# Two 256-column products against one 512-column product in the MLPs of a two-layer hybrid transformer

## The chip, the cores and the metric

The kernel runs on one NeuronCore of a Trainium2 chip. The metric is the device time of one execution in microseconds, the median over runs. A profile is one execution taken by the hardware profiler; its span runs from the first to the last instruction.

## The reference

256 tokens of width 2048 pass two layers. Layer 0 is a stick-breaking attention and an MLP, layer 1 a sparse attention (compressed, selected and windowed keys with gates) and an MLP. Each sublayer adds to the residual. The change concerns the MLPs alone:

```python
def sqrelu_mlp(h, w1, w2):
    return jnp.square(jax.nn.relu(h @ w1)) @ w2

h = h + sqrelu_mlp(rms_norm(h, mlp_norm_g[layer]), mlp_w1[layer], mlp_w2[layer])
```

w1 is 2048 x 8192 and w2 8192 x 2048, all in float32.

## The kernel before

Every large product keeps float32's accuracy by splitting both operands into a high and a low part in fp32r: (hi + lo)(hi + lo) without lo times lo, so three products per tile. Weights come in chunks of two contraction tiles (KC = 2, 256 rows) by 512 columns (NB). `load` (line 130) issues one DMA of 512 KB on SP's queue into one of five raw buffers; `split` has ScalarE copy the chunk to hi (line 123) and VectorE subtract to lo (line 125), four buffers each. TensorE then works on the chunk.

There are two forms. `chunk_N` (line 145) has the activations as the stationary side, 128 x 128, and 512 columns of the weights moving past: 4 tiles per chunk, 12 products of 512 columns. `chunk_T` (line 162) has the weights as the stationary side and the 256 tokens moving past: 8 tiles per chunk (2 contraction tiles by 4 blocks m of 128 columns), first hi against xhi and hi against xlo for each tile, then lo against xhi for each: 24 products of 256 columns. Its four blocks m share two PSUM banks. Every product loads its stationary side anew.

`mlp` (line 290) runs, for each of four quarters fg of the hidden width, four blocks fb of 512 hidden columns through `proj_T` (eight chunks of `chunk_T`) and evacuates each block: ReLU on ScalarE (line 303), square on VectorE (305), the high part yhi on ScalarE (308), the low part ylo on VectorE (309). Then four blocks nb of 512 output columns go through `chunk_N` with w2 (eight chunks each), and `add_h` (line 259) adds them to the residual h. The norm's factor goes in there, squared; its gain went into x.

PSUM has two pools of four banks: acc for these products, att for attention and for the transposes of `make_x` (line 201), which makes xhi (line 206) and xlo (208) from the residual. `out_proj` (line 272) stands ahead of each MLP, leaves its last blocks in acc banks, adds them with `add_h` (line 257), and spawns `next_x`, which makes the MLP's x; its last parts are made between the MLP's first chunks.

The order of instructions on each engine is fixed at compile time by a planner that takes them by the program's order as their inputs and buffers come free in its own reckoning; only the first products of layer 0 are ordered by hand. On the chip each engine takes its instructions in that order. `pump` lets pieces of spawned work in between the halves of a chunk.

Of the kernel before, what the change touches and what calls it, by code (L numbers as in the profile page):

```python
# [15 lines left out]
P = 128  # L16
T = 256
# [22 lines left out]
def hybrid_kernel(  # L40
# [15 lines left out]
    # The residual stream, and the contraction operands in two exact parts each.  # L56
    h = cpool.tile([P, NT, D], F32, name="h")
    xhi = cpool.tile([P, KD, T], F32R, name="xhi")
    xlo = cpool.tile([P, KD, T], F32R, name="xlo")
# [3 lines left out]
    # Gains on the partitions: rows of the norms' gains, then of the head norms.  # L63
# [5 lines left out]
    # x in parts, each loaded behind the weights' chunk before it  # L69
# [68 lines left out]
    def bank(pool, tag):  # L138
        return pool.tile([P, NB], F32, tag=tag, name=tag)

    def chunk_N(ps, src, k0, n0, first, last, ahi, alo, koff=0, by_token=False):
        """ps[t][tok, 512] += a[k, tok]^T w[k, 512] for KC contraction tiles."""
        hi, lo = src if isinstance(src, tuple) else load_split(src, k0, KC, n0, NB)
        tiles = [(kk, k0 - koff + kk, t) for kk in range(KC) for t in range(NT)]
        mm = lambda a, b, k, t, s, e: nc.tensor.matmul(ps[t], a[:, k, t * P:(t + 1) * P], b, start=s, stop=e)  # L145
        for part in [[x for x in tiles if x[2] == t] for t in range(NT)] if by_token else [tiles]:
            for kk, k, t in part:
                mm(ahi, hi[:, kk, :], k, t, first and kk == 0, False)
                mm(alo, hi[:, kk, :], k, t, False, False)
            pump()  # L150
            for kk, k, t in part:
                mm(ahi, lo[:, kk, :], k, t, False, last and kk == KC - 1)
            pump()

    def chunk_T(ps, src, k0, n0, first, last):
        """ps[m // 2][n, (m % 2, tok)] += w[k, n]^T x[k, tok] for four blocks m of 128 columns."""
        hi, lo = src if isinstance(src, tuple) else load_split(src, k0, KC, n0, NB)
        tiles = [(kk, m) for kk in range(KC) for m in range(NB // P)]

        def mm(w, x, kk, m, s, e):  # L160
            o = ps[m // 2][:, (m % 2) * T:(m % 2 + 1) * T]
            nc.tensor.matmul(o, w[:, kk, m * P:(m + 1) * P], x[:, k0 + kk, :], start=s, stop=e, skip_group_check=True)  # L162

        for kk, m in tiles:
            mm(hi, xhi, kk, m, first and kk == 0 and m % 2 == 0, False)
            mm(hi, xlo, kk, m, False, False)
        pump()
        for kk, m in tiles:
            mm(lo, xhi, kk, m, False, last and kk == KC - 1)
        pump()  # L170

    def proj_N(src, n0):
        ps = [bank(acc, "acc") for _ in range(NT)]
        for k0 in range(0, KD, KC):
            chunk_N(ps, src, k0, n0, k0 == 0, k0 + KC == KD, xhi, xlo)
        return ps
# [7 lines left out]
    def split_evac(hi, lo, src, scale=None):  # L184
        """hi + lo = src (times a per-partition factor), src in PSUM."""
        if scale is None:
            nc.scalar.activation(hi, src, AF.Copy)  # L187
            nc.vector.tensor_tensor(lo, src, hi.bitcast(F32), op=OP.subtract)  # L188
        else:
            nc.scalar.activation(hi, src, AF.Copy, scale=scale)  # L190
            nc.vector.scalar_tensor_tensor(
                lo, src, scale, hi.bitcast(F32), op0=OP.mult, op1=OP.subtract
            )

# [1 line left out]
    def make_x(kp, g0):  # L196
        """x of the contraction tiles kp, kp + 1."""
        ps = bank(att, "att")
        for j in range(2):
            for t in range(NT):  # L200
                nc.tensor.transpose(  # L201
                    ps[:, j * T + t * P:j * T + (t + 1) * P], h[:, t, (kp + j) * P:(kp + j + 1) * P], ident
                )
        gain = lambda j: gT[:, g0 + kp + j:g0 + kp + j + 1]
        for j in range(2):
            nc.scalar.activation(xhi[:, kp + j, :], ps[:, j * T:(j + 1) * T], AF.Copy, scale=gain(j))
        for j in range(2):
            nc.vector.scalar_tensor_tensor(
                xlo[:, kp + j, :], ps[:, j * T:(j + 1) * T], gain(j), xhi[:, kp + j, :].bitcast(F32),
                op0=OP.mult, op1=OP.subtract,  # L210
            )
# [3 lines left out]
    def ssq(layer, i, n):  # L215
        """The squares of part i of n of the residual's columns."""
# [9 lines left out]
    def next_x(layer, nb, g0):  # L226
        """Behind the residual's block nb: the next layer's x and sum of squares."""
        ssq(layer, nb, D // NB)
        for kp in range(nb * (NB // P), (nb + 1) * (NB // P), 2):
            yield  # L230
            make_x(kp, g0)
# [14 lines left out]
    def bcast_rows(rstd):  # L246
        """[tok] on the partitions -> the same row [tok] on every partition, in PSUM."""
# [13 lines left out]
    def add_out(nb, ps, scale, ov):  # L261
        """The last block goes out in parts, the tokens that are done first before the others."""
# [9 lines left out]
    def out_proj(src, layer, g0):  # L272
        """h += y w: the last heads' part of the first two blocks comes behind the others'."""
# [16 lines left out]
    def mlp(l, layer, junk, done, last=None):  # L290
        w1, w2 = mlp_w1[l], mlp_w2[l]
        r2 = None
        for fg in range(DFF // D):
            for fb in range(D // NB):
                ps = proj_T(w1, fg * D + fb * NB)
# [4 lines left out]
                for b in range(2):  # L300
                    k = fb * (NB // P) + 2 * b
                    r = junk.tile([P, NB], F32, tag="relu", name="relu")
                    nc.scalar.activation(r, ps[b], AF.Relu)
                    s = junk.tile([P, NB], F32, tag="sq", name="sq")
                    nc.vector.tensor_tensor(s, r, r, op=OP.mult)
                    hi = yhi[:, k:k + 2, :].rearrange("p k t -> p (k t)")
                    lo = ylo[:, k:k + 2, :].rearrange("p k t -> p (k t)")
                    nc.scalar.activation(hi, s, AF.Copy)
                    nc.vector.tensor_tensor(lo, s, hi.bitcast(F32), op=OP.subtract)  # L309
            for nb in range(D // NB):  # L310
                end = last is not None and fg == DFF // D - 1 and nb == D // NB - 1
                ps = [bank(acc, "acc") for _ in range(NT)]
# [10 lines left out]
    # ================= layer 0: stick-breaking attention =================  # L323
    with tc.tile_pool(name="sbp", bufs=2) as sp:
# [11 lines left out]
        # The first products, with x made beside them: every engine in the order given here.  # L336
# [27 lines left out]
        def evac(dst, ps, i):  # L364
            """dst[d, head, tok] = ps times the factors of q (i = 0) or k (i = 1)."""
# [14 lines left out]
        def causal(ap, n):  # L380
            """Keep where key (partition) < query, else 0; ap is [P, n, P]."""
# [5 lines left out]
        def attention(hg, qT, kT, v):  # L387
            for hp in range(0, HG, 2):
                # Keys on the partitions; z0 of keys 0-127 for all queries, z1 of keys 128-255 for
                # queries 128-255; two heads beside each other.  # L390
# [17 lines left out]
                for i in range(2):  # L408
                    # softplus(z) = max(z, 0) + ln(1 + exp(-|z|)); log_sigmoid(z) = min(z, 0) - ln(...)
# [72 lines left out]
    # ================= layer 1: native sparse attention =================  # L482
    # Four selected blocks of 64 are the whole sequence and the window is wider than it, so both
    # branches see every key up to the query. Keys of a group: two parts of 128 selected, 128 window
    # and 8 compressed keys; queries 0-127 see the first part alone.
    with tc.tile_pool(name="nsa", bufs=2) as ap, ExitStack() as last:
# [13 lines left out]
        # Minus the distances of queries (partitions) and keys, NEG where a key is not seen.  # L500
# [10 lines left out]
        for t in range(NT):  # L511
            for a in range(t + 1):
                # CS n + CL - 1 - query, for the compressed keys n from a CH
# [7 lines left out]
        # The last of the 2 CH columns is no key.  # L521
        nc.gpsimd.memset(dist[1][:, 1, 2 * P + NCMP - CH:], NEG)

        def compress(i, cT):
# [24 lines left out]
            # gelu(a) = a / (1 + exp(-2 sqrt(2/pi) (a + 0.044715 a^3)))  # L549
# [39 lines left out]
        def heads(pv, t, n):  # L589
            """The n heads [tok, n, d] of rstd * pv, normed."""  # L590
# [11 lines left out]
        def heads_T(hn, n):  # L602
            """Transposed: [d, n, tok], in PSUM."""
# [18 lines left out]
        def scores(g, j, t, q, khi, klo, sums):  # L622
            """exp of head j's biased scores less their maxima, and the sums, of the three branches."""
# [22 lines left out]
        def scale(g, t, pr, sums):  # L646
            """Each branch's gate over its sum, into its probabilities."""
# [12 lines left out]
        def values(g, t, pr, v):  # L660
            """The sum over the branches of p v, keys on the partitions."""
# [73 lines left out]
        # gates: the last 128 columns, of which the last 48 are the gates  # L735
# [24 lines left out]
        # Queries before the end of the first compressed block see none of them.  # L760
# [5 lines left out]
        # the columns of one group: its selected keys and values, its window keys and values  # L766
# [66 lines left out]
```

## Time and profile before

| what | value |
|---|---|
| median of 3 runs | 2268.32 us (2268.23 to 2268.54) |
| span of the profiled execution | 2265.5 us, 34377 instructions |
| TensorE products busy | 2254.0 us, 99%, 13972 products |
| weight loads busy (overlap the products) | 2014.3 us, 89% |
| VectorE busy | 1245.8 us, 55% |
| ScalarE busy | 1071.5 us, 47% |
| HBM traffic | 178 GB/s over the span |

Busy time of TensorE is modelled at the products' ends, so products overlap in the records; what tells their pace is the length of a run of products over their number. A releaser in square brackets in the timeline names what ended the idle time ahead of an instruction. The profiled execution's own time is not given apart from its span; the median of the runs stands 2.8 us above the span.

### The profile page before, as it was taken

What the parts mean: (1) busy time and instruction counts of PE and PEld (TensorE: products, weight loads), DVE (VectorE), ACT (ScalarE), POOL (GpSimd) and SP (SyncE); (2) the same over time, 40 slices, a digit from 0 to 9 for tenths busy, and PEclk for the clock granted to TensorE, in tenths of its full rate; (3) what the DMA queues carried; (4) which work ended last, traced back from release to release, by engine and by line L of the source; (5) the groups of instructions that cost most, each with busy time, mean ns of one, the idle gap of its engine ahead of it and who ended that gap; (6) DMA issues with size and microseconds to landing.
All of it is one profiled execution on the core that took longest, in us unless ns stands there. A gap on an engine that the chain in (4) does not pass through costs nothing.

```text
span 2265.5 us, 34377 instructions
## 1 busy us (share of the span) xinstructions
PE 2254.0 (99%) x13972; PEld 2014.3 (89%) x13972; DVE 1245.8 (55%) x1515; ACT 1071.5 (47%) x1467; POOL 43.1 (2%) x75
## 2 busy tenths in 40 slices
PE   8999999999999999999999999999999999999999
PEld 8999988998998898898898888889989988988987
DVE  5555555555555455555555777755554555554554
ACT  6555565443444344344433666654434443443442
POOL 0000000000000000000000011000000000000000
PEclk9999999999999999999999999999999999999999
DMA  7555545655655665665566544445556656656654
GB/s 244 179 164 169 167 167 180 178 186 191 184 183 189 185 184 187 188 185 187 184 188 199 148 144 135 137 161 184 186 186 188 185 187 186 186 186 187 186 197 137
DMA packets 244375, 406.17 MB, mean 179 GB/s; under 512 B 13172, under 2 KB 59128, under 8 KB 244216
## 3 DMA queue, kind: packets, MB, share of 16 engines
q1 hardware_dynamic: 243432, 403.53, 57.0%
q8 instruction: 109, 1.79, 0.3%
q10 hardware_dynamic: 784, 0.45, 0.1%
q14 instruction: 50, 0.41, 0.0%
HBM read 401.83 MB, written 2.10 MB: 178 GB/s over the span
## 4 chain that ended last, share of the span: by engine, by line
PE 99%; DMA 0%; DVE 0%; SPq 0%; issue 0%; DVEq 0%
PE acc L145 51%; PE acc L162 43%; PE att L682 1%; PE att L201 1%; PE att L543 1%; PE att L674 0%; PE att L675 0%; PE att L676 0%; PE att L442 0%; PE att L394 0%; PE att L628 0%; PE att L630 0%; PE att L629 0%; DMA h<-in_x_dram 0%; PE att L606 0%; PE att L395 0%
## 5 line engine op out<-in xcount | busy, mean ns | idle before, releaser
L125 DVE TENSOR_TENSOR lo<-raw,hi 128x1024 fp32r<-128x1024 f32 x754 | 922.0, 1224 | 853.2 <-ACT hi L123 840.5
L123 ACT ACTIVATE hi<-raw 128x1024 fp32r<-128x1024 f32 x754 | 799.1, 1060 | 1116.1 <-PE acc L145 572.3
L162 PE MATMUL acc<-xhi,hi 128*128 128x256 f32 x2688 | 659.0, 283 | 0.0
L162 PE MATMUL acc<-xlo,hi 128*128 128x256 f32 x2688 | 656.8, 282 | 0.0
L162 PEld LDWEIGHTS acc<-xlo,hi 128*128 128x128 f32 x2688 | 508.1, 189 | 0.5
L162 PEld LDWEIGHTS acc<-xhi,hi 128*128 128x128 f32 x2688 | 507.9, 189 | 0.6
L145 PE MATMUL acc<-hi,yhi 128*128 128x512 f32 x1280 | 507.9, 397 | 0.0
L145 PE MATMUL acc<-hi,ylo 128*128 128x512 f32 x1280 | 503.9, 394 | 0.0
L162 PE MATMUL acc<-xhi,lo 128*128 128x256 f32 x2688 | 375.7, 282 | 0.0
L145 PE MATMUL acc<-lo,yhi 128*128 128x512 f32 x1280 | 350.9, 395 | 0.0
L162 PEld LDWEIGHTS acc<-xhi,lo 128*128 128x128 f32 x2688 | 343.7, 189 | 0.0
L145 PEld LDWEIGHTS acc<-hi,yhi 128*128 128x128 f32 x1280 | 241.0, 188 | 56.5 <-ACT yhi L187 0.2
L145 PEld LDWEIGHTS acc<-lo,yhi 128*128 128x128 f32 x1280 | 240.3, 188 | 56.3 <-issue 0.4
L145 PEld LDWEIGHTS acc<-hi,ylo 128*128 128x128 f32 x1280 | 241.0, 188 | 54.3 <-DVE ylo L188 0.2
L145 PE MATMUL acc<-hi,xhi 128*128 128x512 f32 x384 | 153.1, 399 | 0.0
L145 PE MATMUL acc<-hi,xlo 128*128 128x512 f32 x384 | 151.5, 395 | 0.0
L145 PE MATMUL acc<-lo,xhi 128*128 128x512 f32 x384 | 106.8, 400 | 0.0
L145 PEld LDWEIGHTS acc<-hi,xhi 128*128 128x128 f32 x384 | 72.4, 188 | 15.8 <-ACT hsq L592 0.2
L145 PEld LDWEIGHTS acc<-hi,xlo 128*128 128x128 f32 x384 | 72.4, 188 | 15.3
L145 PEld LDWEIGHTS acc<-lo,xhi 128*128 128x128 f32 x384 | 70.0, 189 | 15.1 <-issue 1.1
L259 DVE SCALAR_TENSOR_TENSOR h<-acc,r,h 128x512 f32<-128x512 f32 x62 | 43.7, 746 | 36.4 <-PE acc L145 36.4
L309 DVE TENSOR_TENSOR ylo<-sq,yhi 128x512 fp32r<-128x512 f32 x64 | 41.2, 685 | 0.0
(182 smaller groups left out, 985.1 us busy)
## 6 DMA issues: line engine op xcount, KB each, us to landing
raw<-in_mlp_w_dram SPq DMA_DIRECT2D x512, 512.0 KB, 3.7
raw<-in_sb_w_qkv_dram SPq DMA_DIRECT2D x96, 512.0 KB, 3.7
raw<-in_nsa_w_in_dram SPq DMA_DIRECT2D x50, 512.0 KB, 3.5
raw<-in_sb_w_out_dram SPq DMA_DIRECT2D x32, 512.0 KB, 3.7
raw<-in_nsa_w_in_dram SPq DMA_DIRECT2D x64, 256.0 KB, 3.2
raw<-in_nsa_w_out_dram SPq DMA_DIRECT2D x32, 512.0 KB, 3.5
w1t<-in_nsa_cmp_w_dram SPq DMA_DIRECT2D x8, 512.0 KB, 4.1
h<-in_x_dram SPq DMA_DIRECT2D x8, 256.0 KB, 7.8
```

Of the source, the lines that this page charges most:

```text
L123: nc.scalar.activation(hi, raw, AF.Copy)
L125: nc.vector.tensor_tensor(lo, raw, hi.bitcast(F32), op=OP.subtract)
L145: mm = lambda a, b, k, t, s, e: nc.tensor.matmul(ps[t], a[:, k, t * P:(t + 1) * P], b, start=s, stop=e)
L162: nc.tensor.matmul(o, w[:, kk, m * P:(m + 1) * P], x[:, k0 + kk, :], start=s, stop=e, skip_group_check=True)
L201: nc.tensor.transpose(ps[:, j * T + t * P:j * T + (t + 1) * P], h[:, t, (kp + j) * P:(kp + j + 1) * P], ident)
L259: nc.vector.scalar_tensor_tensor(hb, ps[t], scale[:, t:t + 1], hb, op0=OP.mult, op1=OP.add)
L309: nc.vector.tensor_tensor(lo, s, hi.bitcast(F32), op=OP.subtract)
L543: nc.tensor.matmul(ph[:, :GC], w1t[:, l - l0, :], blk[:, l, :, :].rearrange("p g n -> p (g n)"), start=l == 0, stop=l == CL - 1,)
L682: nc.tensor.transpose(ptp[:w, j * P:(j + 1) * P], src(j), ident)
```

## The change

xhi and xlo become the halves of one tile xs, `[P, KD, 2, T]`, so that for each contraction tile the 256 tokens of the high part and the 256 of the low part adjoin. In `mlp`, `proj_T` gives way to `proj_T2`: for each of the 8 tiles of a chunk one product of hi against the 512 adjoining columns, then for each tile lo against xhi into the first half of the same bank. A block now takes four banks, one for each m, with hi·xhi + lo·xhi in the first 256 columns and hi·xlo in the last. Blocks take them from acc and att in turn. The evacuation copies the last half on ScalarE, adds it to the first on VectorE, takes ReLU and square in one VectorE operation, and splits into yhi and ylo as before. In w2's stage the last two blocks of the first three quarters take att banks. The attentions keep the old forms.

```diff
-    xhi = cpool.tile([P, KD, T], F32R, name="xhi")
-    xlo = cpool.tile([P, KD, T], F32R, name="xlo")
+    xs = cpool.tile([P, KD, 2, T], F32R, name="xs")
+    xhi, xlo = xs[:, :, 0, :], xs[:, :, 1, :]
...
+    def proj_T2(ps, src, n0):
+        for k0 in range(0, KD, KC):
+            hi, lo = load_split(src, k0, KC, n0, NB)
+            tiles = [(kk, m) for kk in range(KC) for m in range(NB // P)]
+            for kk, m in tiles:
+                nc.tensor.matmul(
+                    ps[m], hi[:, kk, m * P:(m + 1) * P], xs[:, k0 + kk, :, :].rearrange("p a t -> p (a t)"),
+                    start=k0 + kk == 0, stop=k0 + kk == KD - 1, skip_group_check=True,
+                )
+            pump()
+            for kk, m in tiles:
+                nc.tensor.matmul(
+                    ps[m][:, :T], lo[:, kk, m * P:(m + 1) * P], xhi[:, k0 + kk, :],
+                    start=False, stop=k0 + kk == KD - 1, skip_group_check=True,
+                )
+            pump()
...
-                ps = proj_T(w1, fg * D + fb * NB)
+                ps = [bank(*((acc, "acc"), (att, "att"))[fb % 2]) for _ in range(NB // P)]
+                proj_T2(ps, w1, fg * D + fb * NB)
...
-                    r = junk.tile([P, NB], F32, tag="relu", name="relu")
-                    nc.scalar.activation(r, ps[b], AF.Relu)
-                    s = junk.tile([P, NB], F32, tag="sq", name="sq")
-                    nc.vector.tensor_tensor(s, r, r, op=OP.mult)
-                    hi = yhi[:, k:k + 2, :].rearrange("p k t -> p (k t)")
-                    lo = ylo[:, k:k + 2, :].rearrange("p k t -> p (k t)")
-                    nc.scalar.activation(hi, s, AF.Copy)
-                    nc.vector.tensor_tensor(lo, s, hi.bitcast(F32), op=OP.subtract)
+                    c = junk.tile([P, 2, T], F32, tag="part", name="part")
+                    a = junk.tile([P, 2, T], F32, tag="pre", name="pre")
+                    for j in range(2):
+                        nc.scalar.activation(c[:, j, :], ps[2 * b + j][:, T:], AF.Copy)
+                        nc.vector.tensor_tensor(a[:, j, :], ps[2 * b + j][:, :T], c[:, j, :], op=OP.add)
+                    s = junk.tile([P, 2, T], F32, tag="sq", name="sq")
+                    nc.vector.scalar_tensor_tensor(s, a, 0.0, a, op0=OP.max, op1=OP.mult)
+                    nc.scalar.activation(yhi[:, k:k + 2, :], s, AF.Copy)
+                    nc.vector.tensor_tensor(ylo[:, k:k + 2, :], s, yhi[:, k:k + 2, :].bitcast(F32), op=OP.subtract)
...
-                ps = [bank(acc, "acc") for _ in range(NT)]
+                pool = (att, "att") if nb >= 2 and fg < DFF // D - 1 else (acc, "acc")
+                ps = [bank(*pool) for _ in range(NT)]
```

## Rows read from the trace of the kernel before

**Rows 1.** The page's first part: busy time of each engine, its share of the span, its number of instructions.

```profile
PE 2254.0 (99%) x13972; PEld 2014.3 (89%) x13972; DVE 1245.8 (55%) x1515; ACT 1071.5 (47%) x1467; POOL 43.1 (2%) x75
```

**Rows 2.** The chain that ended last, in order of time, from 405 us to the end of the first MLP and for the second MLP: start, length, what ran, how many instructions. L162 is the T form (w1), L145 the N form (w2).

```profile
406.15 5.89 PE acc L162 x48
...
412.48 2.84 PE acc L162 x24
...
415.76 82.60 PE acc L162 x696
498.36 89.22 PE acc L145 x384
587.58 92.16 PE acc L162 x768
679.74 89.60 PE acc L145 x384
769.33 92.16 PE acc L162 x768
861.49 89.23 PE acc L145 x384
950.72 91.14 PE acc L162 x768
...
1546.21 82.58 PE acc L162 x696
1628.79 89.22 PE acc L145 x384
1718.01 92.16 PE acc L162 x768
1810.17 89.60 PE acc L145 x384
1899.77 92.16 PE acc L162 x768
1991.92 89.23 PE acc L145 x384
2081.15 91.14 PE acc L162 x768
2172.29 89.23 PE acc L145 x384
```

**Rows 3.** Busy time of each engine in two stages of the first MLP (w1 and w2 of quarter 1): window, length, then busy time and instructions of PE, of the weight loader (PEld), DVE, ACT and POOL, the granted clock, the DMA engines' share, GB/s.

```profile
587.58:679.74 92.16, 92.16 (x769) 92.16 (x769) 47.57 (x46) 40.05 (x45) 0.00 (x0) 1.00 0.59 183
679.74:769.33 89.59, 89.59 (x386) 72.08 (x386) 45.75 (x43) 35.89 (x37) 0.00 (x0) 1.00 0.59 188
```

**Rows 4.** Groups of instructions by line, shapes kept apart: line, engine, operation, tiles, shapes, count, busy us, mean ns of one, idle time before them. The evacuation of an MLP block as it is, then the operations on PSUM nearest to the new ones.

```profile
L309 DVE TENSOR_TENSOR ylo<-sq,yhi 128x512 fp32r<-128x512 f32 x64 | 41.2, 685 | 0.0
L305 DVE TENSOR_TENSOR sq<-relu 128x512 f32<-128x512 f32 x64 | 41.2, 684 | 0.0
L308 ACT ACTIVATE yhi<-sq 128x512 fp32r<-128x512 f32 x64 | 36.3, 615 | 0.0
L303 ACT ACTIVATE relu<-acc 128x512 f32<-128x512 f32 x64 | 34.1, 585 | 0.0
L208 DVE SCALAR_TENSOR_TENSOR xlo<-att,gT,xhi 128x256 fp32r<-128x256 f32 x64 | 27.9, 477 | 2.1 <-ACT xhi L206 2.1
L206 ACT ACTIVATE xhi<-att,gT 128x256 fp32r<-128x256 f32 x64 | 26.9, 472 | 10.8 <-PE att L201 10.8
...
L187 ACT ACTIVATE yhi<-att 128x512 fp32r<-128x512 f32 x16 | 9.4, 590 | 4.1 <-PE att L443 2.6 <-PE att L676 1.5
...
L636 DVE TENSOR_REDUCE mx<-p 128x2 f32<-128x256 f32 x16 | 6.5, 409 | 0.0
...
L411 DVE SCALAR_TENSOR_TENSOR s<-att,e 128x512 f32<-128x512 f32 x8 | 5.5, 692 | 24.9 <-ACT e L406 24.9
...
L190 ACT ACTIVATE khi<-att,gT 128x128 fp32r<-128x128 f32 x16 | 5.2, 362 | 2.5 <-DVE klo L191 2.5
```

**Rows 5.** The timeline at the end of an MLP block: start, length, engine, line, operation, tiles, how many, and in brackets the idle time before and what ended it.

```profile
609.38 1.03 PEld L162 LDWEIGHTS acc<-xhi,lo 128*128 128x128 f32 x8
609.49 1.12 PE L162 MATMUL acc<-xhi,lo 128*128 128x256 f32 x8
609.69 1.06 ACT L123 ACTIVATE hi<-raw 128x1024 fp32r<-128x1024 f32 x1 [1.82 <-PE acc L162]
...
610.78 1.23 DVE L125 TENSOR_TENSOR lo<-raw,hi 128x1024 fp32r<-128x1024 f32 x1 [1.65 <-ACT hi L123]
```

**Rows 6.** The waits of SP's queue, the longest in total: us, times, longest.

```profile
SPq L130 <- DVE lo L125: 1700.3, 691, 7.6
```

**Rows 7.** The page's DMA issues: what, how many, KB each, us from issue to landing.

```profile
raw<-in_mlp_w_dram SPq DMA_DIRECT2D x512, 512.0 KB, 3.7
```

**Rows 8.** The timeline where each MLP begins: the addition to the residual (L257) and the first product of w1, for MLP 0 and then MLP 1.

```profile
405.75 1.29 DVE L257 TENSOR_TENSOR h<-acc,h 128x512 f32<-128x512 f32 x2 [0.94 <-PE acc L145]
...
406.08 0.39 PE L162 MATMUL acc<-xhi,hi 128*128 128x256 f32 x1
...
1536.60 1.29 DVE L257 TENSOR_TENSOR h<-acc,h 128x512 f32<-128x512 f32 x2 [1.17 <-PE acc L145]
1536.63 0.28 PE L162 MATMUL acc<-xhi,hi 128*128 128x256 f32 x1
```

## The prediction

> **What bounds the kernel now.** I read the page's busy line first: TensorE (PE) is busy 2254.0 of 2265.5 us, while VectorE (DVE) has 55% and ScalarE (ACT) 47% [rows 1]. A busy PE need not be a PE at its pace, so the chain in order of time comes next. Each MLP is an unbroken run of TensorE work: per quarter of the hidden width a stage of 768 products of 256 columns (w1) and a stage of 384 products of 512 columns (w2), one directly behind the other [rows 2]. In these stages the start-to-start time is a stage's length over its count. w1: 92.16 / 768 = 120.0 ns in quarters 1 and 2, and 91.14 / 768 = 118.67 ns in quarter 3 (82.60 / 696 = 118.68 in the unbroken part of quarter 0), in both MLPs alike. w2: 89.22 / 384 = 232.34 ns in five of the seven stages that run unbroken, 89.60 / 384 = 233.33 ns in the other two. The granted clock is 1.00 in the two stages shown (of two levels, the full 2.4 GHz), and TensorE never idles [rows 3]. So an MLP takes time only through the number of products and the price of each; other engines matter only if they make TensorE wait.
>
> **Part 1: two products become one.** Per MLP there are 4 quarters x 4 blocks x 8 chunks x 8 tiles = 1024 tiles, each now with three 256-column products. The first two (w1's high part with x's high, then its low part) become one of 512 columns; the third stays. In both MLPs 4096 products of 256 columns go and 2048 of 512 come, and 2048 weight loads go. The columns streamed are the same, so the gain is what a product costs beside its columns. The trace has no 512-column product of this form; the nearest row is w2's, with the same tile sizes and data types, a new weight load before each product and 512 adjoining columns. Now: pairs cost 2 x 118.67 = 237.3 ns in quarters 0 and 3, 2 x 120.0 = 240.0 ns in 1 and 2. With 256 pairs a quarter that is 60.75 + 61.44 + 61.44 + 60.75 = 244.4 us an MLP. Then: 1024 x 232.34 ns = 237.9 us. I take 232.34 as five of seven w2 stages show it. Gain 6.5 us an MLP, **12.9 us** for two. Bounds: with 233.33 ns for all, 238.9 us an MLP, so the gain is 10.9 us. The 2048 remaining 256-column products go on at the pace they have; were all at 118.67 or all at 120.0, it would be 1.4 us (1024 x 1.33 ns) less or more. Part 1 alone lies between 9.5 and 14.3 us.
>
> What else could set the pace: the weight loader is busy in all of the 92.16 us of a w1 stage, but in 72.08 of 89.59 us of a w2 stage [rows 3]. If loads of 189 ns, which overlap, set the 120 ns, the third products keep it, except where a load is pulled ahead under a 512-column product. I put at most the difference to the bare columns there: 256 / 2.4 = 107 ns, so 12 ns for one product in each of 256 chunks, 3 us, on the fast side.
>
> The Trainium skill, TensorE: Matmul & The Clock Gate, section Back-to-back issue gap, gives N / 2.4 + 2.5 ns per product at the full clock, 109 ns for 256 columns and 216 for 512. By that a pair saves only 2.5 ns, 5.1 us in all by an estimate from the page. The rows stand higher at both sizes (119 to 120 and 232 to 233) and their difference is 4.0 to 7.7 ns, so the measurement decides for the larger saving.
>
> **Part 2: the evacuation of a block.** Now: two ReLU copies on ACT (585 ns), two squares on DVE (684), two ACT copies to yhi (615), two DVE subtractions to ylo (685) [rows 4]. After: ACT copies four half banks of 256 columns; DVE adds them to the other halves (4 x 256 columns), takes ReLU and square at once (2 x 512), and the last two pairs stay. A 256-column ACT copy out of PSUM lies between 362 ns (128 columns) and 590 (512), so 438 by columns; the nearest row, 256 columns with a scale, says 472. A 256-column DVE operation on PSUM: 477 ns for three operands, 409 for a reduction; I take 450. The fused square: 692 ns at most, by a three-operand row on PSUM [rows 4], as the old one. ACT gets 4 x 0.44 - 2 x 0.585 = 0.6 us more a block, DVE 4 x 0.45 = 1.8 us, 32 blocks each. Cost on the path: none, as long as weight splits keep their lead, since the same two engines make every chunk's hi and lo, in order.
>
> That lead: at 609.69 us ACT starts a hi split, released by the end of a chunk's hi products at 609.4 [rows 5]. With four buffers it is for the chunk four further on, whose hi products begin after the lo products and three chunks of 2.88 us, at 619.1. ACT is done at 610.75, so 8.3 us of cover; DVE's lo split, done at 612.0 and needed 1.9 us later still, has 9.0. A chunk afterwards takes 8 x 0.232 + 8 x 0.12 = 2.82 us. DVE then has 1.23 for the split, so the block's evacuation of 1.8 + 1.4 + 1.4 = 4.6 us delays the next lo splits by at most some 3 us, of 9.0, and is caught up in three chunks. ACT's new copies wait for the block's last products, behind them in the queue stands the next hi split, and TensorE waits for that only if it is 8 us late. DMA: weights come through five raw buffers, each freed by its lo split (SP waits for DVE there, 1700 us in sum); landing takes 3.7 us [rows 6, 7]. A lo split late by 3 us starts a load 3 us late that is wanted five chunks later (14 us). Hidden too.
>
> The last block's y is needed at the seventh of eight chunks of the first w2 block, 6 x 2.8 = 16.7 us later. Hidden.
>
> **Part 3: four PSUM banks for a block in place of two.** Blocks alternate between acc and att, so a bank is asked for again two blocks (45 us) after; w2's blocks in quarters 0 to 2 alternate too. Where this doesn't help is an MLP's first block: out_proj's last block has just left two of the four acc banks, and these come free only with the residual's addition. In MLP 1 that runs from 1536.60 for 1.29 us; the new block starts at 1536.63 [rows 8]. Its third and fourth products would start at 1537.10 and 1537.33; the banks come free near 1537.3 and 1537.95. That is 0.6 us of waiting. In MLP 0 (addition 405.75 to 407.04, first product 406.08 [rows 8]) 0.3 us. Before, the two older banks hid this. Cost **1.0 us**; bounds 0 (if products of the next tile are ordered ahead of the waiting ones) and 2.4 (if the block waits for both additions). In the added waits, matmuls queued behind on PE are all of that same block.
>
> Part 4: xhi and xlo as halves of one tile change only strides; add_h, make_x and the other products keep their sizes. The attention of layer 1 is ordered by a compile-time planner and has holes of its own; a shift of a few instructions may move it 2 us either way, 0 taken.
>
> **Sum.** -12.9 + 1.0 = -11.9 us on the span of 2265.5, so 2253.6. The median of the runs, 2268.32, stands 2.8 us above the span; 2253.6 + 2.8 = **2256.4 us**.
>
> **Rivals.**
> A, within 0.2%: a 512-column product is dearer where the weights are the stationary side than in w2, so that joining saves only a small fixed part. At the worst end of part 1 (9.5) less the worst of part 3 (2.4) and 2 of part 4, 5.1 us are left, 2263.2; each further nanosecond in a 512-column product takes 2 us, so near 2265. For it: no row of this form exists. Against it: w2's price holds in all seven unbroken stages, 2688 products. The skill's fixed cost, above, also lands there (about 2264.2 with part 3). Chance 0.09.
>
> B, slower: TensorE waits at each of the 32 block ends, since a bank is asked for before copy and add have left it, which happens if a pool's four banks are not all free when its turn comes (att is shared with make_x). The wait is then a copy and an add, 0.44 + 0.45 us, and 32 x 0.89 = 28.5 us makes it 2285. It decides from (11.9 + 4.5) / 32 = 0.51 us per block on. Against it: the other pool was left two blocks ago, and make_x runs in the first chunks of the first blocks only. Chance 0.05.
>
> C, faster than the forecast: the third products gain as well, 3 us, and the first blocks don't wait: 2252.4. Chance 0.12, within my range.
>
> The forecast has 0.74. **Range**: down to 2251.0 (C, and a part of the 2 us of part 4), up to 2262.0 (10.9 - 1.4 - 2.4 of gain is 2261.2, with a part of the 2 us); A and B lie outside. About 0.2%, 4.5 us, is what a measurement of this kernel can tell from no change: forecast and C are faster by more, 0.86; A 0.09; B 0.05.
>
> **What the profile after should show.** A w1 stage of 512 products in 90.2 us (59.5 for 256 of 512 columns, 30.7 for 256 of 256), w2 stages unchanged, weight loader under 100% in w1. Products 13972 - 2048 = 11924. DVE up by some 58 us, ACT by some 19. Short waits of TensorE only at the start of each MLP. Wrong if w1 stages hold idle time of TensorE at block ends (B), if the 512-column products start over 236 ns apart (A), or if layer 1's attention changes its length by more than 2 us.

## The result and the profile after

The changed kernel takes 2253.38 us (median of 4 runs, 2252.97 to 2254.51) against 2268.28 us for the kernel before (4 runs, 2267.53 to 2268.54): ratio 0.9935, 95% interval 0.9923 to 0.9947, so 14.9 us faster where 11.9 were forecast. The profiled execution has a span of 2251.2 us, 14.3 less than before; it took 2252.97 us.

The page's first part, to be laid beside [rows 1]:

```profile
PE 2239.2 (99%) x11924; PEld 1909.1 (85%) x11924; DVE 1285.7 (57%) x1643; ACT 1079.4 (48%) x1531; POOL 43.1 (2%) x75
```

2048 products and as many weight loads are gone. VectorE and ScalarE have more to do, and TensorE is as full as it was: a shorter time at the same 99%, because what went is products, not idle time.

The windows of the stages of MLP 0 (w1 of quarter 0, w2 of quarter 0, w1 and w2 of quarter 1, and so on to w1 of quarter 3), columns as in [rows 3], then layer 1's attention and the first stage of MLP 1:

```profile
406.35:497.35 91.00, 91.00 (x522) 79.56 (x522) 53.01 (x66) 43.54 (x58) 0.70 (x1) 1.00 0.63 185
497.35:586.58 89.23, 89.23 (x386) 72.36 (x385) 47.01 (x47) 36.22 (x39) 0.00 (x0) 1.00 0.62 189
586.58:676.49 89.91, 89.91 (x513) 78.48 (x513) 51.27 (x58) 40.70 (x51) 0.00 (x0) 1.00 0.63 187
676.49:765.71 89.22, 89.22 (x385) 72.36 (x385) 47.01 (x47) 36.20 (x39) 0.00 (x0) 1.00 0.62 189
765.71:855.62 89.91, 89.91 (x513) 78.49 (x513) 51.27 (x58) 40.71 (x51) 0.00 (x0) 1.00 0.64 188
855.62:944.84 89.22, 89.22 (x385) 72.34 (x385) 47.00 (x47) 36.20 (x39) 0.00 (x0) 1.00 0.62 189
944.84:1034.75 89.91, 89.91 (x513) 78.49 (x513) 51.27 (x58) 40.71 (x51) 0.00 (x0) 1.00 0.64 187
...
1126.70:1529.60 402.90, 402.58 (x2176) 337.17 (x2176) 271.42 (x522) 225.49 (x471) 24.15 (x19) 1.00 0.56 160
1529.60:1620.53 90.93, 90.93 (x521) 79.30 (x521) 53.07 (x65) 43.76 (x59) 0.69 (x1) 1.00 0.63 185
```

Against [rows 2, 3]: w1 of quarters 1 and 2 went from 92.16 to 89.91 us, of quarter 3 from 91.14 to 89.91. In quarter 0 the whole stage, from the MLP's first product to w2's first, was 92.21 us (406.15 to 498.36) and in MLP 1 92.00 (1536.79 to 1628.79); now 91.00 and 90.93. Over both MLPs that is 4 x 2.25 + 2 x 1.23 + 1.21 + 1.07 = 13.7 us. w2 of quarter 1 went from 89.60 to 89.22 in both, 0.8 us together. MLP 0's first product comes 0.2 us later in this execution (406.35 against 406.15). 13.7 + 0.8 - 0.2 = 14.3 us, the whole difference of the spans. Layer 1's attention is as long as before: 402.93 us there, 402.90 now. The windows of before for it and for the first stage of MLP 1:

```profile
1133.86:1536.79 402.93, 402.61 (x2177) 337.30 (x2177) 271.35 (x522) 225.50 (x471) 24.16 (x19) 1.00 0.53 160
1536.79:1628.79 92.00, 92.00 (x778) 92.00 (x777) 49.36 (x53) 43.03 (x53) 0.70 (x1) 1.00 0.60 184
```

The weight loader is now busy for 78.48 of 89.91 us of a w1 stage, where before it had no gap.

Inside a stage, the chain in order of time at the start of quarter 1 (start, length, what ran, how many):

```profile
586.57 1.86 PE acc L179 x8
588.43 0.95 PE acc L185 x8
589.38 1.86 PE acc L179 x8
591.24 0.94 PE acc L185 x8
```

Eight joined products take 1.86 to 1.87 us (232 to 234 ns each), eight third products 0.94 to 0.95 (118 to 119 ns), a chunk 2.81 us.

The evacuation, in groups of instructions (columns as in [rows 4]):

```profile
L328 DVE SCALAR_TENSOR_TENSOR sq<-pre 128x512 f32<-128x512 f32 x64 | 43.9, 686 | 0.0
L330 DVE TENSOR_TENSOR ylo<-sq,yhi 128x512 fp32r<-128x512 f32 x64 | 43.9, 686 | 0.0
L329 ACT ACTIVATE yhi<-sq 128x512 fp32r<-128x512 f32 x64 | 40.2, 627 | 2.5
...
L326 DVE TENSOR_TENSOR pre<-att,part 128x256 f32<-128x256 f32 x64 | 24.1, 418 | 0.0
L326 DVE TENSOR_TENSOR pre<-acc,part 128x256 f32<-128x256 f32 x64 | 24.0, 418 | 0.0
...
L325 ACT ACTIVATE part<-acc 128x256 f32<-128x256 f32 x64 | 19.0, 383 | 0.0
```

A copy takes 383 ns (438 was estimated), an addition 418 (450). Of TensorE's waits the whole list is three rows, and none is in an MLP:

```profile
PE pgt L370 <- DMA g<-in_sb_norm_g_dram: 6.0, 1, 6.0
PE att L220 <- DMA h<-in_x_dram: 1.6, 1, 1.6
PE att L773 <- DVE gs L770: 0.3, 1, 0.3
```

Last, where MLP 1 begins, the timeline against [rows 8]:

```profile
1529.44 2.14 PE L179 MATMUL acc<-xs,hi 128*128 128x512 f32 x8
...
1530.15 1.00 PEld L179 LDWEIGHTS acc<-xs,hi 128*128 128x128 f32 x5 [0.29 <-DVE h L276]
...
1531.42 0.87 PE L185 MATMUL acc<-xs,lo 128*128 128x256 f32 x6
```

The first eight joined products take 1.98 us from start to start, 0.11 more than the 1.87 of a later chunk; in MLP 0 as well. The order in the compiled program tells why so little. For this chunk the planner took the blocks m in the order 0, 1, 0, 2, 1, 2, 3, 3 in place of 0, 1, 2, 3, 0, 1, 2, 3: the first occupied bank is wanted fourth and the second one seventh. Only the fourth weight load waits for the addition to the residual (L276), for 0.29 us.

### The profile page after: what moved, and what is told of

Same layout as the page of the kernel before. It is cut to its first block, busy times and chain, and to the rows that moved or that the text cites. A ratio compares the mean times of both kernels' runs of the same rounds, so it can differ in the third digit from the quotient of the medians.

```text
span 2251.2 us, 30477 instructions
## 1 busy us (share of the span) xinstructions
PE 2239.2 (99%) x11924; PEld 1909.1 (85%) x11924; DVE 1285.7 (57%) x1643; ACT 1079.4 (48%) x1531; POOL 43.1 (2%) x75
## 4 chain that ended last, share of the span: by engine, by line
PE 99%; DMA 0%; DVE 0%; SPq 0%; issue 0%; DVEq 0%
PE acc L145 40%; PE att L145 12%; PE acc L179 11%; PE att L179 11%; PE acc L162 10%; PE att L185 5%; PE acc L185 5%; PE att L704 1%; PE att L220 1%; PE att L565 1%; PE att L696 0%; PE att L697 0%; PE att L698 0%; PE att L464 0%; PE att L416 0%; PE att L650 0%
## 5 line engine op out<-in xcount | busy, mean ns | idle before, releaser
L145 PE MATMUL acc<-hi,yhi 128*128 128x512 f32 x896 | 355.5, 397 | 0.0
L145 PE MATMUL acc<-hi,ylo 128*128 128x512 f32 x896 | 353.1, 394 | 0.0
L179 PE MATMUL acc<-xs,hi 128*128 128x512 f32 x1024 | 259.6, 395 | 0.0
L179 PE MATMUL att<-xs,hi 128*128 128x512 f32 x1024 | 259.1, 395 | 0.0
L145 PE MATMUL acc<-lo,yhi 128*128 128x512 f32 x896 | 245.8, 395 | 0.0
L179 PEld LDWEIGHTS acc<-xs,hi 128*128 128x128 f32 x1024 | 184.0, 188 | 34.7 <-DVE h L276 0.3
L179 PEld LDWEIGHTS att<-xs,hi 128*128 128x128 f32 x1024 | 183.6, 188 | 33.9
L145 PEld LDWEIGHTS acc<-hi,yhi 128*128 128x128 f32 x896 | 168.8, 188 | 38.3 <-ACT yhi L206 0.2
L145 PEld LDWEIGHTS acc<-lo,yhi 128*128 128x128 f32 x896 | 168.1, 188 | 39.0 <-issue 0.4
L145 PEld LDWEIGHTS acc<-hi,ylo 128*128 128x128 f32 x896 | 168.8, 188 | 37.8 <-DVE ylo L207 0.2
L145 PE MATMUL acc<-hi,xs 128*128 128x512 f32 x768 | 196.8, 397 | 0.0
L145 PEld LDWEIGHTS acc<-hi,xs 128*128 128x128 f32 x768 | 142.2, 188 | 31.2 <-ACT hsq L614 0.2
L162 PE MATMUL acc<-xs,hi 128*128 128x256 f32 x1280 | 168.0, 284 | 0.0
L162 PEld LDWEIGHTS acc<-xs,hi 128*128 128x128 f32 x1280 | 159.0, 190 | 0.3
L145 PE MATMUL att<-hi,ylo 128*128 128x512 f32 x384 | 151.5, 395 | 0.0
L145 PE MATMUL att<-hi,yhi 128*128 128x512 f32 x384 | 151.4, 394 | 0.0
```

Source lines behind the costliest of these rows:

```text
L179: nc.tensor.matmul(ps[m], hi[:, kk, m * P:(m + 1) * P], xs[:, k0 + kk, :, :].rearrange("p a t -> p (a t)"), start=k0 + kk == 0, stop=k0 + ...
```

## The experiments

The theory: a product has a cost beside its columns, and 2048 of these costs are gone; the evacuation and the bank changes lie beside the products and cost nothing. The rivals: the gain comes from banks, layout or order; weight loads set the pace; the evacuation costs something that a larger gain hides.

**e1_apart: everything but the joining.**

```diff
-                nc.tensor.matmul(
-                    ps[m], hi[:, kk, m * P:(m + 1) * P], xs[:, k0 + kk, :, :].rearrange("p a t -> p (a t)"),
-                    start=k0 + kk == 0, stop=k0 + kk == KD - 1, skip_group_check=True,
-                )
+                for i, xp in enumerate((xhi, xlo)):
+                    nc.tensor.matmul(
+                        ps[m][:, i * T:(i + 1) * T], hi[:, kk, m * P:(m + 1) * P], xp[:, k0 + kk, :],
+                        start=k0 + kk == 0 and i == 0, stop=k0 + kk == KD - 1, skip_group_check=True,
+                    )
```

> All of the change stays (four banks a block, acc and att in turn, the new evacuation, xs) but each 512-column product of w1 is again two of 256 columns, with the same weights loaded twice, into the two halves of the bank. Theory (the gain is the cost that a product has beside its columns, 4 to 8 ns a pair): the w1 stages go back from 89.9 to 91.1 to 92.2 us, the products to 13972, and the time to 2266 to 2270 us, that of the kernel before within 0.1%. Rival (the gain comes from the banks, the layout of xs or the order of instructions): it stays within 3 us of 2253.4.

Measured: 2268.47 us, ratio to the kernel before 1.0002 (0.9992 to 1.0011). Windows of w1 of quarter 1, w2 of quarter 1, w1 of quarters 2 and 3:

```profile
588.40:680.55 92.15, 92.15 (x769) 92.15 (x769) 51.28 (x58) 40.74 (x51) 0.00 (x0) 1.00 0.62 184
680.55:770.15 89.60, 89.60 (x387) 72.09 (x386) 46.97 (x47) 36.13 (x39) 0.00 (x0) 1.00 0.59 188
770.15:862.31 92.16, 92.16 (x769) 92.16 (x769) 51.28 (x58) 40.69 (x51) 0.00 (x0) 1.00 0.61 183
...
951.53:1042.67 91.14, 91.14 (x770) 91.14 (x769) 51.27 (x58) 40.71 (x51) 0.00 (x0) 1.00 0.62 186
```

The lengths are those of before to 0.01 us, even the longer w2 stage, with VectorE busy 51.3 us in place of 47.6. The gain is the joining's; banks, layout and evacuation together cost and bring nothing that can be measured.

**e2_acc_only: four banks a block without the second pool.**

```diff
-                ps = [bank(*((acc, "acc"), (att, "att"))[fb % 2]) for _ in range(NB // P)]
+                ps = [bank(acc, "acc") for _ in range(NB // P)]
```

> The joined products, but every block of w1 takes its four banks from acc, of which there are four, so that a block must wait for the evacuation of the one before. This is rival B of the prediction, made to happen. Theory (a wait of a copy and an add, 0.38 + 0.42 us by the trace of after, at 32 block ends): 2253.4 + 32 x 0.8 = 2279 us, with idle time of TensorE at each block end; up to 2300 if it waits for the whole evacuation of the second bank too. Rival (the planner orders other products ahead and hides it): under 2258 us.

Measured: 2341.63 us, ratio 1.0323 (1.0302 to 1.0343), 88 us over the changed kernel and above the theory's 2279 to 2300 us: 2.76 us for each of 32 blocks. The chain at one block's end:

```profile
619.50 1.07 ACT hi L123
...
620.59 1.22 DVE lo L125
621.82 0.35 DVE pre L326
...
622.21 2.22 PE acc L179 x6
```

My price of a copy and an addition left out what stands before them in their engines' queues: ScalarE has a hi split of a later chunk ahead of the copies, VectorE that chunk's lo split ahead of the additions. The waits of TensorE's products:

```profile
PE acc L179 <- DVE pre L326: 43.2, 24, 1.8
PE acc L145 <- DVE pre L326: 14.4, 8, 1.8
```

That is 32 waits of 1.8 us, 57.6 us. The windows around two of them (before the first wait, the wait, behind it, later, the second wait, behind it) show where more goes:

```profile
608.00:619.70 11.70, 11.70 (x69) 10.22 (x69) 4.90 (x4) 4.44 (x5) 0.00 (x0) 1.00 0.64 184
619.70:622.20 2.50, 0.71 (x6) 0.51 (x5) 1.61 (x3) 1.95 (x5) 0.00 (x0) 1.00 0.72 205
622.20:626.60 4.40, 4.39 (x16) 3.78 (x17) 2.84 (x6) 1.01 (x2) 0.00 (x0) 0.61 0.43 125
626.60:645.40 18.80, 18.80 (x107) 16.30 (x107) 9.18 (x8) 7.56 (x8) 0.00 (x0) 1.00 0.58 167
645.40:648.30 2.90, 1.10 (x10) 0.90 (x8) 1.63 (x3) 2.15 (x5) 0.00 (x0) 1.00 0.61 186
648.30:651.20 2.90, 2.90 (x16) 2.54 (x17) 2.82 (x6) 0.85 (x2) 0.00 (x0) 1.00 0.58 180
```

Behind the first wait the granted clock is 0.61, part of the time at the lower of the two levels, and the chunk takes 4.45 us (622.21 to the next chunk's start at 626.66). Behind the second it stays at 1.00, and the chunk takes 2.93 (648.28 to 651.21). The chain shows what a wait costs in all, as the distance from the product that ends one wait to the product that ends the next:

```profile
622.21 2.22 PE acc L179 x6
...
648.28 1.67 PE acc L179 x6
...
672.82 1.71 PE acc L179 x6
```

Without a wait a block takes 89.91 / 4 = 22.5 us. From 622.21 to 648.28 it is 26.1, from 648.28 to 672.82 it is 24.5. Behind the 24 waits that stand inside the w1 stages there are only these two distances: 13 of 24.5 us, where a wait costs 2.0 us (the 1.8 and a little at the new start), and 11 of 26.1, where it costs 3.6, the clock's fall included. These make 66 of the 88 us; the eight waits ahead of w2 are the most of the rest. So rival B's mechanism is real, and at a price three times mine; the alternation of pools is what keeps it away, and the change needs it.

**e3_evac_twice: the new part of the evacuation doubled.**

```diff
-                        nc.scalar.activation(c[:, j, :], ps[2 * b + j][:, T:], AF.Copy)
-                        nc.vector.tensor_tensor(a[:, j, :], ps[2 * b + j][:, :T], c[:, j, :], op=OP.add)
+                        for _ in range(2):
+                            nc.scalar.activation(c[:, j, :], ps[2 * b + j][:, T:], AF.Copy)
+                            nc.vector.tensor_tensor(a[:, j, :], ps[2 * b + j][:, :T], c[:, j, :], op=OP.add)
```

> The four copies and four additions of a block's evacuation are each done twice, some 1.5 us more of ScalarE and 1.7 us of VectorE in each of 32 blocks. Theory (the evacuation lies within the 8 us lead of the weight splits): 2253.4 us within 0.1%, no idle time of TensorE in the w1 stages, VectorE busy some 54 us more. Rival (part of the evacuation is on the path): 10 to 55 us slower.

Measured: 2253.47 us, ratio to the kernel before 0.9934 (0.992 to 0.9949), as the changed kernel. VectorE is busy 1328.3 us, 42.6 more, ScalarE 1111.0, 31.6 more. The evacuation is hidden. (54 us more was expected for VectorE. Instructions that stand back to back overlap in the records: in the changed kernel three additions of 0.42 us each take 1.08.)

**e4_third_halved: smaller products.**

```diff
-                nc.tensor.matmul(
-                    ps[m][:, :T], lo[:, kk, m * P:(m + 1) * P], xhi[:, k0 + kk, :],
-                    start=False, stop=k0 + kk == KD - 1, skip_group_check=True,
-                )
+                for t in range(NT):
+                    nc.tensor.matmul(
+                        ps[m][:, t * P:(t + 1) * P], lo[:, kk, m * P:(m + 1) * P], xhi[:, k0 + kk, t * P:(t + 1) * P],
+                        start=False, stop=k0 + kk == KD - 1, skip_group_check=True,
+                    )
```

> The third product of w1 (lo against xhi, 256 columns) is done as two of 128 columns, each with its weight load. Theory (a product costs about 5 ns beside some 0.444 ns a column, from 118.7 ns at 256 and 232.3 at 512): 61.9 ns each, so a pair is 5 ns dearer, and 2048 pairs make it 2253.4 + 10.9 = 2264 us. Rival (the weight loader sets the pace of small products; it was busy without a gap in the w1 stages of before at one load per 119 to 120 ns): a load and its product every 95 to 119 ns, 2048 pairs dearer by 71 to 119 ns, 2399 to 2497 us.

Measured: 2467.72 us, ratio 1.0878 (1.0857 to 1.09). My theory of one straight line, 61.9 ns for 128 columns, fails for products this small; the time lies where the loader's rival put it. The timeline of one chunk's sixteen third products:

```profile
641.85 1.90 PE L186 MATMUL acc<-xs,lo 128*128 128x128 f32 x16
643.59 0.67 PE L179 MATMUL att<-xs,hi 128*128 128x512 f32 x2
```

Sixteen in 1.74 us, 109 ns each, with half the columns of a product that takes 118.7 ns. The weight loader is busy in all of these 1.74 us. That it sets the 109 ns is the likeliest reading, but not shown by itself: each of these products has its own load, and the loader had no gap either in the w1 stages of before, where products of 256 columns took 118.67 to 120.0 ns. Whether a part of the 118.7 is the load's was still open.

**e5_third_384: the size between.**

```diff
-                    ps[m][:, :T], lo[:, kk, m * P:(m + 1) * P], xhi[:, k0 + kk, :],
+                    ps[m][:, :T + P], lo[:, kk, m * P:(m + 1) * P],
+                    xs[:, k0 + kk, :, :].rearrange("p a t -> p (a t)")[:, :T + P],
```

> The third product of w1 takes 384 columns in place of 256: lo against xhi and the first half of xlo, so that lo times lo comes in for half of the tokens, which the kernel leaves out. It measures a product between the two sizes. A: a product costs a fixed 5 ns and 0.444 ns a column also at 256 columns: 175.4 ns, and 2048 x 56.9 ns = 116 us more, 2370 us. B: beside the columns at 2.4 GHz the cost is a share of the columns (19.2 ns at 512, so 14.4 at 384), and the 256-column product is some 2 ns dearer than that for its weight load: 174.4 ns, 2367 us. The trace's start-to-start times tell A from B, the total doesn't.

Measured: 2373.92 us, ratio 1.0466 (1.0448 to 1.0484). w1 and w2 of quarter 1:

```profile
601.79:706.41 104.62, 104.62 (x513) 93.19 (x513) 51.27 (x59) 41.15 (x53) 0.00 (x0) 1.00 0.54 162
706.41:796.00 89.59, 89.59 (x385) 72.08 (x385) 46.92 (x47) 35.76 (x37) 0.00 (x0) 1.00 0.59 187
```

A pair takes 104.62 / 256 = 408.7 ns. Less 232.3 to 233.3 for the joined product, 175.4 to 176.4 are left for 384 columns. That is nearer to A (175.4) than to B (174.4), but doesn't decide: runs of equal products differ by 1.0 to 1.3 ns between stages without any edit, which is as much as A and B differ by. From 256 to 512 columns the three sizes lie on one line to within a nanosecond or two, some 5 ns and 0.444 ns a column, so the load adds at most that much of its own at 256. Since every product in all these runs has a load of its own, no run tells whether the 5 ns beside the columns belong to the product or to its load; the joining removes both.

**e6_w2_acc: w2's blocks back in acc.**

```diff
-                pool = (att, "att") if nb >= 2 and fg < DFF // D - 1 else (acc, "acc")
+                pool = (acc, "acc")
```

> The change without one of its parts: all blocks of w2 take their banks from acc, as before, so that the first block of w1 in quarters 1 to 3 finds two of its four acc banks just left by w2's last block, as the first block of an MLP does. Theory (the planner orders the next tile's products ahead of the waiting ones; the MLP starts show 0.11 us of waiting each): 6 x 0.11 = 0.7 us more, 2254 us, not to be told from 2253.4. Rival (as the prediction had it for the MLP's start, 0.3 to 0.6 us each): 2 to 4 us more, 2255.5 to 2257.

Measured: 2254.38 us, ratio to the kernel before 0.9938 (0.9925 to 0.9951), which doesn't differ from the changed kernel's. w1 of quarter 1 is 89.95 us in place of 89.91, and six such stages make some 0.2 us; 0.9 of the 1.1 us by which the profiled span is longer is the wait for the input x at the kernel's start (2.5 us against 1.6). So this part of the change brings under half a microsecond in all; the planner's order covers two occupied banks.

**e7_adds_4x: how far the cover goes.**

```diff
-                        nc.vector.tensor_tensor(a[:, j, :], ps[2 * b + j][:, :T], c[:, j, :], op=OP.add)
+                        for _ in range(4):
+                            nc.vector.tensor_tensor(a[:, j, :], ps[2 * b + j][:, :T], c[:, j, :], op=OP.add)
```

> Each of the four additions of a block's evacuation is done four times, so VectorE has 12 x 0.42 = 5.0 us more in each of 32 blocks and is busy some 19 of 22.5 us there. Theory (what counts is the 9 us lead of the lo splits, and the evacuation would delay them by 5 to 8 us): 2253.4 us within 0.1%, VectorE busy 160 us more. Rival (the cover is smaller, as splits and evacuation alternate in the queues in the planner's order): waits of TensorE at block ends, 0.3 us or more each, 2263 us or more.

Measured: 2254.01 us, ratio to the kernel before 0.9937 (0.9924 to 0.9949); VectorE busy 1404.2 us, 118.5 more (160 was expected; the additions overlap in the records). w1 of quarter 1:

```profile
588.20:678.10 89.90, 89.90 (x513) 78.47 (x513) 62.38 (x94) 40.70 (x51) 0.00 (x0) 1.00 0.61 187
```

The stage's length has not moved and TensorE waits nowhere in it. The end of the cover was not reached.

**e8_apart_nudged: the two rhythms.** In the kernel before and in e1, runs of equal products take 120.0 or 118.67 ns each, always in the same quarters. The edit is made on e1:

```diff
+                if fb == 0 and fg > 0:
+                    for _ in range((0, 1 + 2 * l, 2 + 2 * l, 1)[fg]):
+                        nc.tensor.transpose(ps[0][:, :P], ident, ident)
                 proj_T2(ps, w1, fg * D + fb * NB)
```

> The kernel with the products apart (e1), with one to four 128-column transposes of the identity ahead of the first w1 block of quarters 1 to 3: 1, 2 and 1 of them in MLP 0, 3, 4 and 1 in MLP 1; the bank is begun anew behind them, so nothing of the result changes. In e1 as in the kernel before, quarters 1 and 2 run at 120.0 ns a product and quarter 3 at 118.7, in both MLPs. Theory (two rhythms of a run of equal products, and the phase at its start decides between them): some of the six stages change their rhythm, each by 1.0 us; if all came to 118.7, 4.1 us less and 0.7 us from w2, less 14 x 0.11 us for the transposes, 2265.2 us. Rival (the rhythm hangs on something fixed in a quarter, such as addresses): the same rhythm as in e1 in each stage, 2268.5 + 1.5 = 2270.0 us.

Measured: 2267.58 us, ratio to the kernel before 0.9998 (0.9988 to 1.0007). The total doesn't tell it from e1, the windows do (w1 of quarters 1 and 2 of MLP 0, then w1 and w2 of quarter 1 of MLP 1):

```profile
588.32:680.58 92.26, 92.26 (x770) 92.26 (x770) 51.24 (x58) 40.73 (x51) 0.00 (x0) 1.00 0.61 183
...
770.19:861.54 91.35, 91.35 (x771) 91.35 (x770) 51.24 (x58) 40.70 (x51) 0.00 (x0) 1.00 0.62 185
...
1718.28:1810.75 92.47, 92.47 (x772) 92.47 (x771) 51.22 (x58) 40.72 (x51) 0.00 (x0) 1.00 0.61 183
1810.75:1899.99 89.24, 89.24 (x387) 72.31 (x386) 47.01 (x47) 36.20 (x39) 0.00 (x0) 1.00 0.60 189
```

With the transposes' own time in the windows, quarter 2 came from 92.16 to 91.35 us (in MLP 1 likewise), and w2 of quarter 1 in MLP 1 from 89.60 to 89.24. Quarter 1 stayed at the slower rhythm, and quarter 3 at the faster. (The edit adds 4 + 8 = 12 transposes; the expectation counted 14.) Apart from these twelve the compiled program is that of e1 on every engine, in order and addresses. So addresses don't fix the rhythm, and a few transposes, 0.1 us each, ahead of a stage can change it; what decides between the two stays open.

## Why the prediction was right

**What bounds it.** Right. The MLPs were runs of products without a gap, and the joining alone moves the time (e1).

**Part 1, the joined products.** The mechanism is right: 12.9 us forecast for w1, 13.7 measured there after the first blocks' waits. By the forecast a pair of joined and third product takes 232.34 + 120.0 = 352.3 ns in quarters 1 and 2; measured, 89.91 / 256 = 351.2. The third products took the faster rhythm everywhere, 1.2 us over four stages, where I had let them keep their pace; the bound for that stood in the text. That w2 of quarter 1 would come to the faster rhythm too, 0.8 us, I had not seen. e8 changes the rhythm of stages without any joining, by a few transposes ahead of them. So these 2 us needn't come with the joining: they were luck. The forecast at the nearest row, w2's 512-column product, held to 0.5 ns.

The weight loader was the term that I could only bound. By e4 and e5 a 256-column product lies within a nanosecond or two of the line through the larger ones, and only smaller products, 109 ns at 128 columns, stand far above it. The loader's 100% in w1 was therefore no sign that it set the pace, and the 3 us of case C did not come.

**Part 2, the evacuation.** Right: hidden, and so are even 12 more additions a block, 3.7 us more of VectorE's busy time (e7). The added busy time was overestimated: VectorE 39.9 us more (58 forecast), ScalarE 7.9 (19), because the instructions are shorter (418 and 383 ns) and overlap in the records.

**Part 3, the banks.** The term was mis-sized: 1.0 us forecast for the MLPs' first blocks, 0.2 measured. Its lower bound named the reason, products of the next tile ordered ahead; the compiled order does that, and leaves one short wait. The steady alternation was right, and e2 shows what it is worth, 88 us.

**Part 4.** Right: layer 1's attention kept its length to 0.03 us.

**The sum.** 0.8 (banks) + 1.0 (w1's products, with 0.2 lost to slightly longer joined ones) + 0.8 (w2) - 0.2 (the kernel's start) make the 2.4 us between the forecast 11.9 and the span's 14.3. The rest of the 14.9, 0.6 us, comes from setting a median beside one execution. The 2.8 us that the forecast added to the span are not all time around it: in nearly all executions on record, before and after, the time is 1.7 to 1.8 us more than the same execution's own span. By that the profiled execution of before was some 1.0 us faster than its median; the one of after was 0.4 faster (2252.97 against 2253.38).

**The rivals.** A is out: joined products start 232 to 234 ns apart. The page of the Trainium skill, TensorE: Matmul & The Clock Gate, section Back-to-back issue gap, has 2.5 ns of fixed cost beside the columns for a product by itself, by an estimate 5.1 us here. The runs show some 5 ns fixed and 0.444 ns a column, where the page's formula has 0.417, so here the measurement decides. B did not occur, but its price was wrong: 2.76 us a block (e2), not 0.89, as the queues ahead of copy and addition and the clock behind the wait belong to it. Its point of decision, 0.51 us a block, would have been passed at once. C's time, 2252.4 us, is nearer to the measured 2253.38 than the forecast's 2256.4. But only one of its two causes came, the first blocks with hardly a wait (0.8 us); most of the distance is the rhythm's 2 us. The prediction had a bound for the third products' share of it, and a reason for neither share.

## What to carry to other kernels

Where products run without a gap, a 512-column product in place of two 256-column ones was worth 4.8 to 7.5 ns each here, and no more. Splitting 256 columns into two products of 128 was dear: 2 x 109 ns in place of 118.7. Price an undecided shape by the nearest row of the same kernel, and read a busy share of the loader only beside the start-to-start times. Whoever doubles the PSUM that a block needs should first see that the next block has other banks: the wait costs what stands ahead of the evacuation in its engines' queues, and at some block ends the clock as well.

## What the runs showed of the hardware

Runs of equal products keep one of two rhythms, 118.67 or 120.0 ns at 256 columns and 232.34 or 233.33 at 512, over a whole stage; the same stages keep the same one in the kernel before and in e1. Transposes of a tenth of a microsecond each, ahead of a stage, changed it in three stages of e8, with the same order and addresses otherwise. A product of 128 columns with its own weight load took 109 ns (e4), nearly as long as one of 256 columns. Behind an idle time of TensorE of 1.8 us the granted clock was 0.61 over 4.4 us at one block's end and 1.00 behind the next, so the same wait cost 3.6 us in one place and 2.0 in another (e2).
